# The matrices of a state-space layer, made two groups at a time: moved ahead of the stage that uses them

## The chip, the cores and the metric

One core of a Trainium2 chip runs the kernel. A core has five engines that each work through a queue of their own in order: TensorE (PE in the profile; its weight loads are PEld), VectorE (DVE), ScalarE (ACT), GpSimd (POOL) and SyncE (SP), which here mostly issues DMA transfers. They meet by semaphores. The metric is the device time of one execution in microseconds (us); less is better.

## What is computed

One layer of a decoder with 2048 positions of 1024 channels, in float32. The projection `P = rms_norm(x) @ W_in` feeds two attention mixers (columns a, b, c below) and a diagonal state-space mixer (columns u), and an output projection and a feed-forward block follow. The change lies in the projection and in the state-space mixer:

```python
A_bar = jnp.exp(A * dt)                       # 32 groups of 16 channels, 64 complex states each
B_bar = ((A_bar - 1.0) / A)[..., None] * Bm
Bu = jnp.einsum('blgp,gnp->blgn', uf.astype(jnp.complex64), B_bar)
_, states = lax.associative_scan(_scan_combine, (a_seq, Bu), axis=1)
y = jnp.einsum('blgn,gpn->blgp', states, Cm).real
y = y + d_skip.astype(f32).reshape(SSM_GROUPS, SSM_GROUP_CH) * uf
z = jax.nn.gelu(y.reshape(Bsz, L, W))
```

The kernel cuts the 2048 positions into 128 blocks of 16. Within a block the answer is a product with a lower triangular Toeplitz matrix of `C A^t B` (the local part); across blocks only the state at a block's edge is scanned, and it enters the answer through the matrices `C A^t`, t = 0 to 16.

## The kernel before

`phase_front` (L81) makes the projection. The positions are taken as 16 slices s of 128 rows; half 0 does s = 0 to 7, half 1 does 8 to 15. For a slice `load_h` (L99) loads x, transposes it on TensorE (tile pt, L111), splits it into a high and a low part (hh on ScalarE L113, hl on VectorE L114), squares x on ScalarE (L117, after which x's buffer is free; there are two) and makes the slice's row factor r, 1 over the root of the mean square, by `rsqrt_steps` (L41): eight instructions of 128x1, on GpSimd. `load_w` (L128) loads a chunk's weights and splits each of 8 parts into wh (ScalarE, L143) and wl (VectorE, L144). `product` (L150) then runs 24 matmuls for one slice and chunk (`mm3`: wh hh, wl hh, wh hl for 8 parts). ScalarE takes the result out with the factor r.

There are five chunks of columns: two of u (256 columns each), then a, b, c. In half 0 all five run, and beside u's second chunk to c the tables of the state-space part are made in 13 parts (`ssm_tables`, VectorE above all; AR and AI are the powers of A, C1 and C2 the coefficients C after a transposition on TensorE, tile p, L414; Ea and Eb the factors for turning states). In half 1 the two u chunks run first, so that u is complete; then a, b, c run merged with the state-space steps.

Those steps (`ssm_steps`, L430) treat the 32 groups as 16 pairs b. For a pair:

- `outer` (L460): CA = AR x C1 + AI x C2, 128x544, three GpSimd instructions L465 to L467;
- `local` (L470): pk, two matmuls of CA with the table Yp (L476); VectorE adds D (kst, L479), ScalarE copies the rest (L480), and SP stores kst to DRAM as a strip, dkp (L481), from which the Toeplitz matrix Wc is read back, shifted line by line (L490);
- `turned` (L483): the turns (six VectorE instructions L453 to L458 on t2u, into the factors E), B's matrices Bp (L494 to L496, VectorE), transposes of u (pu) and of Bp (pbt) on TensorE, and ScalarE's copies U and BT (L503, L508);
- `scanned` (L518): pv = BT times U on TensorE (L524), its halves swapped by ScalarE (vs, L515 and L516), m and the scan Q on VectorE (L527 to L533), the swap of Q on ScalarE (again L515 and L516), the states St on GpSimd (t, St, L536 and L537);
- `answer` (L539): py from Wc, U, CA and St, six TensorE instructions, and the activation into u_st.

CA has three buffers, so GpSimd runs up to two pairs ahead. Within the stage a pair's steps lie between halves of the products of a, b and c: `merge` deals the steps of several lists evenly into one order, and a scheduler then sets each engine's queue from that order, priorities and the buffers that come free. Waits go by semaphores on tiles; a load's wait for a free buffer stands in SP's queue and holds what is behind it.

Of the kernel before, what the change touches and what calls it, by code (L numbers as in the profile page):

```python
# [80 lines left out]
def phase_front(tc, C, x, norm1_g, w_in, u_st, pd, rh_a, prm, dkp, extra):  # L81

    nc = tc.nc
    with ExitStack() as ctx:
# [43 lines left out]
        def load_w(half, kind, c0, n):  # L128
# [301 lines left out]
def ssm_steps(tc, C, S, u_st, dkp, tp, ps, ps_t):  # L430
# [29 lines left out]
    def outer(b):  # L460

        bc = [P, GB, 17, 16]
        CA, t1 = tl(bc, "CA", b, 3), tl(bc, "t1", b)
        ar, ai = (S[n][:, :, of(b)].rearrange("p t g -> p g t").unsqueeze(3).broadcast_to(bc) for n in ("AR", "AI"))
        nc.gpsimd.tensor_tensor(CA, ar, S["C1"][:, of(b)].unsqueeze(2).broadcast_to(bc), op=ALU.mult)  # L465
        nc.gpsimd.tensor_tensor(t1, ai, S["C2"][:, of(b)].unsqueeze(2).broadcast_to(bc), op=ALU.mult)
        nc.gpsimd.tensor_tensor(CA, CA, t1, op=ALU.add)  # L467
        M["c", b] = CA

    def local(b):  # L470
# [1385 lines left out]
```

## Time and profile before

| | us |
|---|---|
| median of 3 runs | 2604.18 (2604.03 to 2604.61) |
| the profiled execution | 2609.15 |
| its span in the trace | 2607.0 |
| front phase (`phase_front`) | 0 to some 441 |
| half 0's chunk c | 144 to 179 |
| half 1's u chunks | 179 to 234 |
| SSM stage: a, b, c of half 1 with the 16 pairs | 234 to 441 |

Over the span TensorE is busy 2487.8 us (95%), VectorE 1802.0 (69%), ScalarE 1328.8 (51%), GpSimd 1141.6 (44%). These shares are means over stages with different limits. Read one stage by what its fullest engine waits for, then follow that wait to the engine that was late, and on that engine look for the instructions that took longer than others of their shape.

### The profile page before, as it was taken

The numbers are of one execution on the slowest core, as the hardware profiler recorded it, in microseconds if no ns is written. First come the engines' busy times: TensorE is split into PE (matmuls) and PEld (weight loads), VectorE is DVE, ScalarE is ACT, GpSimd is POOL, SyncE is SP. The second block draws the span as 40 slices with busy tenths as digits, with TensorE's granted clock in tenths as the row PEclk, the third lists the DMA queues.
The fourth block names the chain that finished last, engine by engine and source line by source line (L and its number), as shares of the span: only waits on it lengthen the run. The fifth ranks groups of instructions, "written<-read, shape, count | busy, mean of one in ns | idle before, by whom it ended". The sixth has DMA issues, their size and how long they took to land. (4 is left out here: it accounts for less than half of the span.)

```text
span 2607.0 us, 38424 instructions
## 1 busy us (share of the span) xinstructions
PE 2487.8 (95%) x12904; PEld 2089.8 (80%) x12904; DVE 1802.0 (69%) x3436; ACT 1328.8 (51%) x2774; POOL 1141.6 (44%) x1195
## 2 busy tenths in 40 slices
PE   8999989999899998999989999899999999999999
PEld 7999888777787777778868878688887888888887
DVE  3836876854776677787665655755557887888886
ACT  5344444854775656566545554544444443344442
POOL 2014544221333223333257666665564354454447
PEclk9999999999899999999989999999999999999999
DMA  4342214321312112112366666665546534444335
GB/s 124 88 140 76 73 51 123 118 76 48 106 56 69 52 49 84 61 52 69 100 198 191 189 197 193 203 182 152 154 134 219 179 115 133 130 128 128 120 102 197
DMA packets 393621, 316.78 MB, mean 122 GB/s; under 512 B 51494, under 2 KB 364460, under 8 KB 391600
## 3 DMA queue, kind: packets, MB, share of 16 engines
q1 hardware_dynamic: 357328, 289.16, 37.1%
q10 hardware_dynamic: 36096, 25.17, 3.0%
q8 instruction: 102, 1.67, 0.3%
q14 instruction: 95, 0.78, 0.1%
HBM read 206.26 MB, written 107.99 MB: 121 GB/s over the span
## 5 line engine op out<-in xcount | busy, mean ns | idle before, releaser
L1341 ACT CAST v<-vr 128x512 fp32r<-128x512 f32 x224 | 139.4, 624 | 307.8 <-DMA vr<-vd 150.0
L1342 DVE TENSOR_TENSOR v<-vr,v 128x512 fp32r<-128x512 f32 x224 | 239.6, 1078 | 77.8 <-ACT v L1341 74.9
L1656 PE MATMUL pdc<-dw,v 128*128 128x512 f32 x768 | 186.7, 392 | 4.9 <-ACT dw L1341 3.0
L1656 PE MATMUL pdb<-dw,v 128*128 128x512 f32 x768 | 184.6, 389 | 0.0
L1656 PE MATMUL pda<-dw,v 128*128 128x512 f32 x768 | 184.5, 389 | 0.0
L1656 PEld LDWEIGHTS pdc<-dw,v 128*128 128x128 f32 x768 | 145.0, 189 | 36.6 <-ACT dw L1341 3.4
L1452 POOL TENSOR_TENSOR fs<-ur,ur 128x512 f32<-128x512 f32 x64 | 94.0, 1469 | 171.5 <-DMA ur<-in_w_up 109.9
L1656 PEld LDWEIGHTS pdb<-dw,v 128*128 128x128 f32 x768 | 144.1, 188 | 30.3 <-ACT v L1341 0.4
L1656 PEld LDWEIGHTS pda<-dw,v 128*128 128x128 f32 x768 | 144.2, 188 | 29.9
L1341 ACT CAST uh<-fs 128x512 fp32r<-128x512 f32 x128 | 78.7, 621 | 150.9 <-PE pub L1481 63.3
L1342 DVE TENSOR_TENSOR ul<-fs,uh 128x512 fp32r<-128x512 f32 x128 | 131.9, 1034 | 22.7 <-ACT uh L1341 22.6
L1342 DVE TENSOR_TENSOR ul<-ur,uh 128x512 fp32r<-128x512 f32 x96 | 101.5, 1060 | 49.8 <-ACT uh L1341 43.5
L1497 POOL TENSOR_TENSOR ev<-e,e 128x512 f32<-128x512 f32 x64 | 98.9, 1545 | 38.5 <-ACT e L1494 23.2
L76 PE MATMUL pw<-wo_h,mh 128*128 128x512 f32 x256 | 110.4, 431 | 5.0 <-DVE ml L1211 2.5
L864 DVE TENSOR_TENSOR tls<-pps,ths 128x512 fp32r<-128x512 f32 (+1 forms) x144 | 92.8, 658 | 29.9 <-ACT ths L863 22.6
L863 ACT CAST ths<-pps 128x512 fp32r<-128x512 f32 (+1 forms) x144 | 79.1, 565 | 57.4 <-PE pps L860 27.5
L1481 PE MATMUL puc<-fl,uh 128*128 128x512 f32 x256 | 101.3, 396 | 4.8 <-DVE fl L1342 4.8
L1481 PE MATMUL pub<-fh,uh 128*128 128x512 f32 x256 | 102.9, 402 | 2.5 <-ACT fh L1341 2.5
L1481 PE MATMUL puc<-fh,uh 128*128 128x512 f32 x256 | 101.5, 397 | 3.9 <-ACT fh L1341 2.5
L77 PE MATMUL pw<-wo_l,mh 128*128 128x512 f32 x256 | 105.2, 411 | 0.0
L78 PE MATMUL pw<-wo_h,ml 128*128 128x512 f32 x256 | 104.8, 410 | 0.0
L1481 PE MATMUL pub<-fl,uh 128*128 128x512 f32 x256 | 102.3, 400 | 1.6 <-DVE fl L1342 1.6
(566 smaller groups left out, 7940.9 us busy)
## 6 DMA issues: line engine op xcount, KB each, us to landing
vr<-vd SPq DMA_DIRECT2D x224, 256.0 KB
ur<-in_w_up SPq DMA_DIRECT2D x128, 256.0 KB
vd<-ev SPq DMA_DIRECT2D x128, 256.0 KB
vd<-e ACTq DMA_DIRECT2D x64, 256.0 KB
dr<-in_w_down SPq DMA_DIRECT2D x32, 512.0 KB
x<-in_x SPq DMA_DIRECT2D x16, 512.0 KB
mx<-in_x SPq DMA_DIRECT2D x16, 512.0 KB
x<-mx ACTq DMA_DIRECT2D x16, 512.0 KB
```

The lines of the kernel that those rows point to most:

```text
L76: nc.tensor.matmul(out, sh, mh, start=first, stop=False)
L77: nc.tensor.matmul(out, sh, ml, start=False, stop=False)
L78: nc.tensor.matmul(out, sl, mh, start=False, stop=last)
L863: nc.scalar.copy(th[:, 0:nb], pt[:, 0:nb])
L864: nc.vector.tensor_tensor(tl[:, 0:nb], pt[:, 0:nb], th[:, 0:nb], op=ALU.subtract)
L1341: nc.scalar.copy(dh, src)
L1342: nc.vector.tensor_tensor(dl, src, dh, op=ALU.subtract)
L1452: nc.gpsimd.tensor_tensor(t, x, y, op=op)
L1481: nc.tensor.matmul(bank[b], w[:, k], h[o][:, k], start=first and k == 0 and n == 0, stop=k == HALF - 1 and n == 2, skip_group_check=True)
L1497: nc.gpsimd.tensor_tensor(tile_("v" + o), x, y, op=op)
L1656: nc.tensor.matmul(bank[b, q], x[:, q, j], y[:, j], start=first and j == 0 and n == 0, stop=j == 1 and n == 2, skip_group_check=True)
```

## The change

`outer` and `local` of all pairs leave `ssm_steps` for a new function, `pair_steps`, of 18 steps. Its first 8 steps (PAIRS_FIRST) are merged with half 0's chunk c, the other 10 with half 1's two u chunks. CA gets tiles of its own (oCA, four buffers) and goes to DRAM (dca, 278 KB a pair), two steps after it was made ("later stores"), as kst does. In the SSM stage `turned` reads CA back by a DMA. The turns of a pair now stand behind Bp, at the end of `turned`. The tables' 13 parts are dealt over u's second chunk, a and b alone, no longer over c too. The row factors of slices 8 to 15 are made on VectorE, not on GpSimd. Half 0's weight splits of a, b, c get a higher priority (W_HOIST).

```diff
-                rsqrt_into(nc, box_x[0], r, ss, 1.0 / D, 1, "rq", nc.gpsimd)
+                rsqrt_into(nc, box_x[0], r, ss, 1.0 / D, 1, "rq", nc.vector if s >= 8 else nc.gpsimd)
...
+                    with tc.high_priority(offset=W_HOIST) if kind in "abc" and not half else nullcontext():
+                        nc.scalar.activation(wh, raw[:, j], AF.Copy, scale=g1[:, k:k + 1])
+                        nc.vector.scalar_tensor_tensor(wl, raw[:, j], g1[:, k:k + 1], wh, op0=ALU.mult, op1=ALU.subtract)
...
-                run(lists[0] + (lists[1] + lists[2][:1] if half else []))
+                run(merge(lists[0] + lists[1], pairs[PAIRS_FIRST:]) + lists[2][:1] if half else lists[0])
...
-                run(merge(sum(lists[1:], []), [lambda: next(gen, None)] * TABLE_PARTS + [lambda: None] * TABLE_REST))
+                run(merge(sum(lists[1:4], []), [lambda: next(gen, None)] * TABLE_PARTS))
+                c_pre = ctx.enter_context(ExitStack())
+                pre = c_pre.enter_context(tc.tile_pool(name="pre", bufs=1, side="right", reuse_waits="tile"))
+                pairs = pair_steps(tc, C, S, dkp, dca, pre, ps_g)
+                run(merge(lists[4], pairs[:PAIRS_FIRST]))
             else:
+                c_pre.close()
...
-TABLE_REST = 3
+PAIRS_FIRST = 8
+W_HOIST = 300
...
+def pair_steps(tc, C, S, dkp, dca, tp, ps):
...
+    def outer(b):
+        bc = [P, GB, 17, 16]
+        CA = M["c", b] = tp.tile(bc, F32, tag="oCA", name=f"oCA{b}", bufs=4)
+        t1 = tp.tile(bc, F32, tag="ot", name=f"ot{b}", bufs=2)
...
+    def local(b):
...
+        kst = M["k", b] = tp.tile([16, GB, 256], F32, tag="kst", name=f"kst{b}", bufs=3)
...
+    def stored(b):
+        nc.sync.dma_start(dca[b], M.pop(("c", b)))
+        nc.sync.dma_start(dkp[group_slice(b), :, 112:368].rearrange("g q c -> q g c"), M.pop(("k", b)))
+
+    res = []
+    for b in range(NB + 2):
+        res.append(lambda b=b: (b > 1 and stored(b - 2), b < NB and outer(b), 0 < b <= NB and local(b - 1)))
+    return res
...
     def turned(b):
 
-        turns(b)
-        CA = M["c", b]
-        Wc = tl([P, GB, 256], "Wc", b, 2)
+        CA, Wc = tl([P, GB, 17, 16], "CA", b, 2), tl([P, GB, 256], "Wc", b, 2)
+        nc.sync.dma_start(CA, dca[b])
...
         M["b", b] = BT, U, CA, Wc
-        if b + 1 < NB:
-            outer(b + 1)
+        turns(b)
...
-    res = [first, lambda: turned(0)]
+    res = [lambda: None, lambda: turned(0)]
     for b in range(NB):
-        res += [lambda b=b: scanned(b), lambda b=b: next_(b)]
+        res += [lambda b=b: scanned(b), lambda b=b: b and answer(b - 1)]
```

The scheduler's result at three places follows; in these rows the line numbers of the kernel after are larger by 1 in the projection, by 7 in the tables and by 20 to 45 in the SSM steps, and the instructions of `outer` have become L452 to L454.

GpSimd in the SSM stage, before, around pairs 1 to 5 (CA and t<-k_AI are the outers; t<-Q and St the states):

```order
L536 TENSOR_TENSOR t_3128<-Q_3123,E_3058 128x4x127
L465 TENSOR_TENSOR CA_3207<-k_AR,k_C_725 128x544
L537 TENSOR_TENSOR St_2906<-t_3128 128x2x127
L467 TENSOR_TENSOR CA_3207<-CA_3207,t_3208 128x544
L466 TENSOR_TENSOR t_3322<-k_AI,k_C_726 128x544
L536 TENSOR_TENSOR t_3242<-Q_3237,E_3177 128x4x127
L465 TENSOR_TENSOR CA_3321<-k_AR,k_C_725 128x544
L537 TENSOR_TENSOR St_2905<-t_3242 128x2x127
L467 TENSOR_TENSOR CA_3321<-CA_3321,t_3322 128x544
L466 TENSOR_TENSOR t_3441<-k_AI,k_C_726 128x544
```

The same engine after, from the last two outers on:

```order
L452 TENSOR_TENSOR oCA_2773<-k_AR,k_C_726 128x544
L454 TENSOR_TENSOR oCA_2773<-oCA_2773,ot_2774 128x544
L452 TENSOR_TENSOR oCA_2886<-k_AR,k_C_726 128x544
L454 TENSOR_TENSOR oCA_2886<-oCA_2886,ot_2887 128x544
L556 TENSOR_TENSOR t_3215<-Q_3210,E_3177 128x4x127
L557 TENSOR_TENSOR St_3118<-t_3215 128x2x127
L556 TENSOR_TENSOR t_3316<-Q_3311,E_3273 128x4x127
L557 TENSOR_TENSOR St_3119<-t_3316 128x2x127
```

An outer's instructions stood between the states of every pair; now they are all done before the first state, and only t and St are left in the stage.

SyncE's queue with half 1's loads of x, before (x_2227 is slice 10, the next ones 11 and 12):

```order
L171 DMA pc<-po_c 128x398
L101 DMA x_2227<-in_x 128x1024
L137 DMA wr_u_4_2619<-in_w_in 128x256
L101 DMA x_2284<-in_x 128x1024
L137 DMA wr_u_5_2625<-in_w_in 128x256
L101 DMA x_2341<-in_x 128x1024
L101 DMA x_2398<-in_x 128x1024
```

And after (x_2351 is slice 10, then 11, 12, 13; oCA_2511 is pair 11, oCA_2607 pair 12, kst_2238 pair 7):

```order
L101 DMA x_2351<-in_x 128x1024
L469 DMA dkp<-kst_2238 16x2x256
L468 DMA dca<-oCA_2511 128x544
L101 DMA x_2408<-in_x 128x1024
L137 DMA wr_u_4_2808<-in_w_in 128x256
L469 DMA dkp<-kst_2348 16x2x256
L468 DMA dca<-oCA_2607 128x544
L101 DMA x_2478<-in_x 128x1024
L137 DMA wr_u_5_2814<-in_w_in 128x256
L101 DMA x_2548<-in_x 128x1024
```

Before, only loads stood between loads of x; now the stores of CA of pair 11 and of kst of pair 7 stand ahead of slice 11's load, those of pairs 12 and 8 ahead of slice 12's, and so on.

VectorE in half 1's first u chunk, before (hl of slices 9 and 10, with two weight splits):

```order
L114 TENSOR_TENSOR hl_2173<-pt_0_2174,hh_2172 128x512
L144 SCALAR_TENSOR_TENSOR wl_u_2_2610<-wr_u_2_2607,g_111,wh_u_2_2609 128x256
L114 TENSOR_TENSOR hl_2173<-pt_1_2181,hh_2172 128x512
L144 SCALAR_TENSOR_TENSOR wl_u_3_2616<-wr_u_3_2613,g_111,wh_u_3_2615 128x256
L114 TENSOR_TENSOR hl_2230<-pt_0_2231,hh_2229 128x512
L114 TENSOR_TENSOR hl_2230<-pt_1_2238,hh_2229 128x512
```

And after (hl of slice 9, the row factors of slices 8 and 9, rqh, rqt and r, and the splits and pk's step between them):

```order
L114 TENSOR_TENSOR hl_2284<-pt_0_2285,hh_2283 128x512
L49 TENSOR_SCALAR r_2217<-rqt,r_2217 128x1
L48 TENSOR_SCALAR rqt<-r_2217,rqh 128x1
L114 TENSOR_TENSOR hl_2284<-pt_1_2292,hh_2283 128x512
L49 TENSOR_SCALAR r_2217<-rqt,r_2217 128x1
L48 TENSOR_SCALAR rqt<-r_2217,rqh 128x1
L44 TENSOR_SCALAR rqh<-ss_2299 128x1
L49 TENSOR_SCALAR r_2217<-rqt,r_2217 128x1
L45 TENSOR_SCALAR r_2301<-rqh 128x1
L145 SCALAR_TENSOR_TENSOR wl_u_2_2799<-wr_u_2_2796,g_112,wh_u_2_2798 128x256
L48 TENSOR_SCALAR rqt<-r_2301,rqh 128x1
L145 SCALAR_TENSOR_TENSOR wl_u_3_2805<-wr_u_3_2802,g_112,wh_u_3_2804 128x256
```

Where VectorE had the hl of one slice after another, eight small instructions of a row factor now come between them, and a kst for a pair. TensorE's queue has a pk (two matmuls) in each c product of half 0 and about one in each slice of the u chunks, and none in the SSM stage, where every pair had one.

## Rows read from the trace of the kernel before

**Rows 1.** Busy time of each engine (with its number of instructions), granted clock of TensorE (1.00 is full speed), busy share of the DMA engines and their GB/s, in four stretches: half 0's chunk c, half 1's first u chunk, the next chunk's start, the SSM stage. Columns: PE busy (x) PEld busy (x) DVE busy (x) ACT busy (x) POOL busy (x), PEclk, DMA share, GB/s.

```profile
144.00:179.00 35.00, 35.00 (x195) 35.00 (x195) 7.67 (x20) 12.61 (x28) 0.00 (x0) 1.00 0.40 126
179.00:211.00 32.00, 30.32 (x255) 29.49 (x254) 12.66 (x22) 22.06 (x45) 18.42 (x64) 1.00 0.41 122
211.00:222.00 11.00, 11.00 (x95) 11.00 (x94) 3.69 (x10) 5.28 (x10) 0.20 (x1) 1.00 0.36 99
234.00:441.00 207.00, 189.26 (x1095) 179.75 (x1094) 155.82 (x291) 90.67 (x195) 94.88 (x75) 0.96 0.25 72
```

**Rows 2.** What TensorE waited for in the SSM stage, 234 to 441 us: its line, the releaser, us in all, times, longest.

```profile
PE pv L524 <- ACT BT L508: 13.6, 7, 4.8
PE pm_a L77 <- DVE wl_a L144: 2.1, 1, 2.1
PE pm_a L76 <- ACT wh_a L143: 2.0, 1, 2.0
```

**Rows 3.** One of these waits, in the order of time, 338 to 348 us (start us, us, engine, line, op, tiles; in brackets the idle time before and what ended it).

```profile
338.77 1.42 POOL L467 TENSOR_TENSOR CA<-CA,t 128x544 f32<-128x544 f32 x1
338.89 1.57 DVE L457 TENSOR_TENSOR t2u<-k_Ea,k_Eb 128x256 f32<-128x256 f32 x1
...
344.24 0.40 ACT L515 COPY Q<-Q 64x256 f32<-64x256 f32 x1 [6.96 <-DVE kst L479]
...
346.80 0.56 ACT L508 COPY BT<-pbt 128x512 f32<-128x512 f32 x1
...
347.41 0.58 PE L524 MATMUL pv<-U,BT 128*128 128x128 f32 x1 [4.85 <-ACT BT L508]
```

**Rows 4.** As group 1, for two short stretches of the SSM stage.

```profile
241.00:248.00 7.00, 5.03 (x18) 4.54 (x18) 2.25 (x5) 3.35 (x7) 0.00 (x0) 0.53 0.41 114
347.00:351.00 4.00, 3.59 (x15) 3.59 (x16) 3.79 (x10) 1.09 (x3) 0.20 (x1) 0.57 0.38 113
```

**Rows 5.** VectorE in order of time, start of the SSM stage: one product of the turns beside GpSimd's outers, a sum of the same shape and a product of 128x512 with GpSimd idle (its L466 from 235.34 lasts 1.24 us).

```profile
222.27 1.40 DVE L454 TENSOR_TENSOR t2u<-k_Ea,k_Eb 128x256 f32<-128x256 f32 x1
...
236.90 0.42 DVE L455 TENSOR_TENSOR E<-t2u 128x256 f32<-128x256 f32 x1
...
238.61 0.69 DVE L495 TENSOR_TENSOR t<-k_AI,k_W 128x512 f32<-128x512 f32 x1
```

**Rows 6.** VectorE's instructions on the tiles t2u and E of the turns (L453 to L458) in the SSM work, 222 to 441 us: span, busy (x), PEclk, DMA share, GB/s.

```profile
222.00:441.00 219.00, 63.51 (x96) 0.96 0.25 70
```

**Rows 7.** VectorE's three instructions of Bp, 222 to 441 us, by line and shape: busy us, mean ns of one, idle time before.

```profile
L494 DVE TENSOR_TENSOR Bp<-k_AR,k_Y 128x512 f32<-128x512 f32 x16 | 17.9, 1119 | 15.8 <-PE pbt L506 15.8
L496 DVE TENSOR_TENSOR Bp<-Bp,t 128x512 f32<-128x512 f32 x16 | 17.4, 1087 | 0.3
...
L495 DVE TENSOR_TENSOR t<-k_AI,k_W 128x512 f32<-128x512 f32 x16 | 12.7, 791 | 0.1
```

**Rows 8.** The same view of GpSimd, 222 to 441 us.

```profile
L467 POOL TENSOR_TENSOR CA<-CA,t 128x544 f32<-128x544 f32 x16 | 24.6, 1538 | 0.6
L536 POOL TENSOR_TENSOR t<-Q,E 128x508 f32<-128x508 f32 x16 | 22.8, 1426 | 106.2 <-ACT Q L516 106.2
L465 POOL TENSOR_TENSOR CA<-k_AR,k_C 128x544 f32<-128x544 f32 x16 | 22.7, 1422 | 10.8 <-DVE gate L201 10.8
L466 POOL TENSOR_TENSOR t<-k_AI,k_C 128x544 f32<-128x544 f32 x16 | 21.1, 1319 | 1.1
L537 POOL TENSOR_TENSOR St<-t 128x254 f32<-128x254 f32 x16 | 15.2, 953 | 0.7
```

**Rows 9.** All instructions that read or write the tiles pk (local products on TensorE, and VectorE's and ScalarE's steps from them to kst), 222 to 441 us: PE busy (x) PEld busy (x) DVE busy (x) ACT busy (x), PEclk, DMA share, GB/s.

```profile
222.00:441.00 219.00, 16.42 (x64) 12.12 (x64) 2.67 (x16) 8.66 (x16) 0.96 0.25 70
```

**Rows 10.** Half 1's loads of x on SyncE's queue, and the transposes on TensorE that wait for x, in order of time.

```profile
186.02 1.07 PE L111 MATMUL pt<-c_ident,x 128*128 128x128 f32 x8 [0.33 <-DMA x<-in_x]
...
188.84 11.84 SPq L101 DMA_DIRECT2D x<-in_x  x4
...
193.81 1.07 PE L111 MATMUL pt<-c_ident,x 128*128 128x128 f32 x8 [0.85 <-DMA x<-in_x]
```

**Rows 11.** What TensorE waited for from 73 to 234 us.

```profile
PE pm_b L77 <- DVE wl_b L144: 1.4, 1, 1.4
PE pt L111 <- DMA x<-in_x: 1.2, 2, 0.8
```

**Rows 12.** A one-operand VectorE instruction of 128x96 at two times: with GpSimd in L466 (319.32 to 320.48), and with GpSimd idle.

```profile
319.39 1.15 DVE L53 TENSOR_SCALAR hnhn<-hnhn 128x96 f32<-128x96 f32 x1
...
321.46 0.21 DVE L53 TENSOR_SCALAR hnhn<-hnhn 128x96 f32<-128x96 f32 x1
```

**Rows 13.** Half 0's chunk b, in order of time: a load of B and its use, the last load of C, C's transposes, and two matmuls of the product.

```profile
124.73 1.36 SPq L385 DMA_DIRECT2D t_B<-in_ssm_b_im  x1
...
129.51 0.34 PE L76 MATMUL pm_b<-wh_b,hh 128*128 128x384 f32 x1
...
129.68 0.34 PE L77 MATMUL pm_b<-wl_b,hh 128*128 128x384 f32 x1
...
129.84 0.42 DVE L397 TENSOR_SCALAR t_B<-t_B 64x512 f32<-64x512 f32 x1 [0.46 <-DMA t_B<-in_ssm_b_im]
129.85 0.51 SPq L393 DMA_DIRECT2D craw<-in_ssm_c_re  x1
...
139.46 1.04 PE L414 MATMUL p<-c_ident,craw 128*128 128x128 f32 x8
```

More of the change, by code (lines that the diff above doesn't have):

```diff
@@ L210, in phase_front @@
                 rest = sum(lists[2:], [])[1:]
-                run(merge(rest, ssm_steps(tc, C, S, u_st, dkp, tp, ps_g, ps_t)))
+                run(merge(rest, ssm_steps(tc, C, S, u_st, dkp, dca, tp, ps_g, ps_t)))
                 store(0)
@@ L427, with group_slice, ssm_steps @@
 GB = 2
-def ssm_steps(tc, C, S, u_st, dkp, tp, ps, ps_t):
+def group_slice(b):
+    return slice(b * GB, b * GB + GB)
+def pair_steps(tc, C, S, dkp, dca, tp, ps):
+    nc = tc.nc
+    M = {}
+    NB = G // GB
+    def outer(b):
+        bc = [P, GB, 17, 16]
+        CA = M["c", b] = tp.tile(bc, F32, tag="oCA", name=f"oCA{b}", bufs=4)
+        t1 = tp.tile(bc, F32, tag="ot", name=f"ot{b}", bufs=2)
+        ar, ai = (S[n][:, :, group_slice(b)].rearrange("p t g -> p g t").unsqueeze(3).broadcast_to(bc) for n in ("AR", "AI"))
+        nc.gpsimd.tensor_tensor(CA, ar, S["C1"][:, group_slice(b)].unsqueeze(2).broadcast_to(bc), op=ALU.mult)
+        nc.gpsimd.tensor_tensor(t1, ai, S["C2"][:, group_slice(b)].unsqueeze(2).broadcast_to(bc), op=ALU.mult)
+        nc.gpsimd.tensor_tensor(CA, CA, t1, op=ALU.add)
+    def local(b):
+        CA = M["c", b]
+        pk = ps.tile([P, GB, 256], F32, tag="pb", name=f"pk{b}", bufs=2)
+        for i in range(GB):
+            g = b * GB + i
+            nc.tensor.matmul(pk[:, i], S["Yp"][:, g:g + 8].rearrange("p a b -> p (a b)"), CA[:, i, 0:16].rearrange("p a b -> p (a b)"),
+                             start=True, stop=True)
+        kst = M["k", b] = tp.tile([16, GB, 256], F32, tag="kst", name=f"kst{b}", bufs=3)
+        nc.vector.tensor_tensor(kst[:, :, 0:16], pk[0:16, :, 0:16], S["dD"][:, group_slice(b)], op=ALU.add)
+        nc.scalar.copy(kst[:, :, 16:256], pk[0:16, :, 16:256])
+    def stored(b):
[5 more added lines that the diff above has]
+    return res
+def ssm_steps(tc, C, S, u_st, dkp, dca, tp, ps, ps_t):
     nc = tc.nc
@@ L437, in ssm_steps @@
     NB = G // GB
+    of = group_slice
     def tl(shape, n, b, bufs=1):
         return tp.tile(shape, F32, tag=n, name=f"{n}{b}", bufs=bufs)
-    def of(b):
-        return slice(b * GB, b * GB + GB)
     def turns(b):
@@ L458, in turns @@
         nc.vector.tensor_tensor(o[1], u1, u2, op=ALU.add)
[L460 to L470, printed above, removed]
-        CA = M["c", b]
-        pk = ps.tile([P, GB, 256], F32, tag="pb", name=f"pk{b}", bufs=2)
-        for i in range(GB):
-            g = b * GB + i
-            nc.tensor.matmul(pk[:, i], S["Yp"][:, g:g + 8].rearrange("p a b -> p (a b)"), CA[:, i, 0:16].rearrange("p a b -> p (a b)"),
-                             start=True, stop=True)
-        kst = tl([16, GB, 256], "kst", b)
-        nc.vector.tensor_tensor(kst[:, :, 0:16], pk[0:16, :, 0:16], S["dD"][:, of(b)], op=ALU.add)
-        nc.scalar.copy(kst[:, :, 16:256], pk[0:16, :, 16:256])
-        nc.sync.dma_start(dkp[of(b), :, 112:368].rearrange("g q c -> q g c"), kst)
     def turned(b):
-        turns(b)
-        CA = M["c", b]
-        Wc = tl([P, GB, 256], "Wc", b, 2)
+        CA, Wc = tl([P, GB, 17, 16], "CA", b, 2), tl([P, GB, 256], "Wc", b, 2)
+        nc.sync.dma_start(CA, dca[b])
         for i in range(GB):
@@ L546, in answer @@
         nc.scalar.activation(u_st[:, of(b)], py, AF.Gelu_apprx_tanh)
-    def first():
-        outer(0)
-        local(0)
-    def next_(b):
-        if b:
-            answer(b - 1)
-        if b + 1 < NB:
-            local(b + 1)
-    res = [first, lambda: turned(0)]
+    res = [lambda: None, lambda: turned(0)]
     for b in range(NB):
-        res += [lambda b=b: scanned(b), lambda b=b: next_(b)]
+        res += [lambda b=b: scanned(b), lambda b=b: b and answer(b - 1)]
         if b + 1 < NB:
```

7 lines of the change are left out of this document (3 added, 4 removed).

## The prediction

> **What bounds the kernel now.** I read the page first (TensorE 95% busy over the span), then the busy time of each engine by stage, then TensorE's waits in the stage that the change touches, then the engines that these waits lead to. The edit lies in the front phase, 0 to 441 us; what follows keeps its instructions, so I only ask when the front phase ends.
>
> The stage table [rows 1] splits it. Half 0's chunk c (144 to 179) has TensorE without a gap and GpSimd without one instruction. Half 1's first u chunk (179 to 211) and second (211 to 222 and on) are TensorE's too. The SSM stage (234 to 441) is different: TensorE is busy 189.26 of 207 us, at a mean granted clock of 0.96. TensorE's waits there [rows 2] sum to 13.6 + 2.1 + 2.0 = 17.7 us, and 13.6 of it is one thing: pv waits for ScalarE's copy BT, 7 times. One of the seven in full [rows 3]: VectorE's state factors (t2u, E) run beside GpSimd's outer products; the product L457 takes 1.57 us while GpSimd is in L467. ScalarE's Q swap has stood still 6.96 us behind the late VectorE, the copy BT stands behind the swap on ScalarE (in order), and pv has waited 4.85 us when it starts.
>
> The clock is the second part. Mean 0.96 over 207 us, with levels 1 and 0.5 of full speed, is 207 x 0.04 / 0.5 = 16.6 us at the lower level (1.2 GHz), so 8.3 us lost. The stretches with 0.53 and 0.57 [rows 4] lie right behind such a wait (347 to 351 starts where pv waited 4.85 us).
>
> Why VectorE is late shows in one op at two times [rows 5]: the sum L455, 128x256, takes 0.42 us when GpSimd is idle; L454, the same shape, takes 1.40 us at 222.27, with GpSimd's outers running back to back. Over the stage the 96 ops of the turns take 63.51 us [rows 6] instead of 96 x 0.42 = 40.3, and the three Bp products [rows 7] 17.9 + 12.7 + 17.4 = 48.0 instead of 48 x 0.69 = 33.1 (L495 with GpSimd idle, [rows 5]): 23.2 + 14.9 = 38 us of VectorE go into waiting for GpSimd.
>
> **The change part by part.** *SSM stage.* The outers (L465 to L467) leave it: 22.7 + 21.1 + 24.6 = 68.4 us of GpSimd, 4.28 a pair [rows 8]; with them go those 38 us of VectorE. What stays on GpSimd is t and St, 22.8 + 15.2 = 38.0 us [rows 8], which can still block VectorE. So VectorE falls from 155.82 of 207 us busy [rows 1] to some 120, and the local product, its addition and its copy (16.42 us TensorE, 2.67 VectorE, 8.66 ScalarE for 16 pairs [rows 9]) leave as well. TensorE becomes the only full engine of the stage. The gain is at most 17.7 + 8.3 = 26.0 us. It isn't all had: the 4.1 us of waits for the first a casts [rows 2] don't come from the outers, and ScalarE still has the swap ahead of BT. I keep a quarter: **-19.6**. Bounds: all of it, -26.0; half of it, -13.0 (the nearest row against me is t and St, over half as long as the outers).
>
> *The local products pk.* 16.42 us of TensorE leave the SSM stage and come back in chunk c (pairs 0 to 7) and the u chunks, where TensorE has no gap [rows 1]: **0** net. Nothing hides them there.
>
> *The outers in their new place.* Eight run beside chunk c, 8 x 4.28 = 34 us in a stretch of 35 in which GpSimd had nothing and VectorE 7.67 us [rows 1]: that is the cover, and pair b is wanted once a c product (35/8 = 4.4 us and its pk), so the pace fits. Eight more run beside u1 and u2. There SP's queue now holds the x loads behind the stores of CA. In u1 TensorE needs 32/8 = 4.0 us a slice [rows 1], its waits for x in it, and now 16.42/16 = 1.0 more for pk, some 4.9; GpSimd needs 4.28 a pair. So the pace fits but the phase is tight: x is used 193.81 - 188.84 = 5.0 us after its issue [rows 10], TensorE already waits 0.33 and 0.85 us for it, and the store of pair 11, 12 x 4.28 = 51 us after the start of the outers at about 137 (C's data near 135, below, then its copies on VectorE), lets slice 11's load go at 188.4, where it went at 188.84. Each late microsecond of the start is one on x. Besides, the u weights' second parts, two-operand VectorE ops, can each wait up to 1.4 us like L454 [rows 5], and hl of slice 8 stands behind six of them. From slice 12 on there is also a loop: x of slice b waits for the store of CA b, that for outer b, that (four buffers) for pk b-4, and TensorE reaches pk b-4 two slices before x of b: 1.0 + 4.28 + 5.0 = 10.3 us for two slices, against TensorE's 9.8, about even. I take **+4**. Bounds: -1.2 (the waits for x vanish, as the pk give each load more time; [rows 11]) and +15 (first rival, in full).
>
> *Row factors on VectorE.* Eight 128x1 ops for each of 8 slices leave GpSimd, 18.42 us for the 64 [rows 1]; GpSimd would else need 4.28 + 2.3 a slice, more than TensorE. On VectorE (12.66 us busy of 32) they add some 64 x 0.2 = 13 us: an estimate from the small op of [rows 12] without GpSimd beside it, 0.21. Covered, if they aren't blocked.
>
> *Tables earlier, b's and c's casts earlier.* Two terms, one on the other. The waits for wl_b (1.4, [rows 11]) may go. But C's transposes, at 139.46 behind the seventh b product, now stand three matmuls into the sixth: 45 matmuls earlier, at 0.17 each [rows 13] 7.7 us, so at 131.8 or, without the waits, 130.4. Their data can't be there: the loads of B and C wait for VectorE's last use of a table's space, which the new order has at the same place. A load of B issued at 124.73 was used at 129.84; the last of C, issued at 129.85, then lands near 135. That is a stall of 3.2 against the old time. I take **+2.5**; bounds -1.4 (the casts' wait gone, C small and early) and +3.2.
>
> *CA through DRAM.* 16 stores and 16 loads of 128x544 (278 KB each). The loads are issued a pair ahead of py; the DMA engines are 25% busy in the stage [rows 1], 41% at most in the stretches shown [rows 4]. **0**, and up to +1 if the first is late; the turns, now behind Bp, are also no longer the first thing that pbt waits for.
>
> **Sum:** -19.6 + 4 + 2.5 = -13.1 against the profiled execution's 2609.15: 2596.0. That execution is 5.0 above the median of the three runs (2604.18), and one execution doesn't tell in which stage, so the difference goes to the median: **2591**.
>
> **Rivals.** *The row factors are blocked in u1.* Beside GpSimd's L466 a one-operand TENSOR_SCALAR of 128x96 took 1.15 us, alone 0.21 [rows 12]. If the 128x1 ops wait like it, each of GpSimd's three ops a pair stops one of them: 3 x 1.4 + 5 x 0.2, two hl at 0.7 and a kst, 6.8 us a slice against TensorE's 4.9, with the hl that TensorE wants queued behind them: 8 x 1.9 = +15 in place of my +4, so -19.6 + 15 + 2.5 = -2, **2602**. For it: that row; against it: one element a partition is a very small transfer, and no row has it beside a long GpSimd op. The Trainium skill (SBUF — State Buffer, "Who interferes with whom") has the same lock on the port pair that VectorE shares with GpSimd, held for a whole instruction, for two-operand ops and for tensor_scalar in its two-port modes; by it this rival would hold wherever such a mode is taken, and the traced 1.15 agrees with it, while no run here shows it for one element. The page also says that whoever issues first holds the pair; by that GpSimd could be the blocked one, and the outers late.
>
> *The waits stay.* BT stays behind the swap on ScalarE and TensorE's stream between pbt and pv stays 12 matmuls long (2.1 us at 0.17), so half of the 26 stays whatever VectorE does: -13 + 6.5 = -6.5, **2598**. Against it: the swap was late because of VectorE's blocked ops [rows 3].
>
> *Slower: the queue of x loads.* The loop above (pk b-4, outer b, store of CA b, x of b, two slices on) sets the pace when its parts stretch: each of the outer's three ops waits for a VectorE op of up to 0.7 (hl), 4.28 + 2.1 = 6.4; x lands in 10 us instead of 5.0 since the stores share its DMA engines; with pk 17.4 for two slices, 8.7 for one, 3.8 over TensorE's 4.9. For slices 10 to 15 that is +23 in place of my +4: -19.6 + 23 + 2.5 = +6, **2610**. It decides from a loop of some 17 us up. For it: TensorE waits for x at two places already, and SP issues in order. Against it: GpSimd's ops hardly stretch beside a full VectorE (the means of [rows 8] are 1.32 to 1.54, in a stage where VectorE is 75% busy), and the DMA engines have room.
>
> That the change doesn't do what it says is excluded by the order: no outer and no pk stands in the SSM stage any more.
>
> **How the numbers follow.** Forecast 2591, chance 0.62; row factors blocked 0.13 (2602); waits stay 0.15 (2598); queue 0.10 (2610). The forecast's best end, all bounds at once, is -26.0 - 1.2 - 1.4 = -28.6: 2575.6; its worst without the rivals -13 + 4 + 3.2 = -5.8: 2598. Rival one lies within 2604, the slow one beyond. **Range 2577 to 2604.** A change of under 0.2% (5.2 us, so 2599.0 to 2609.4) can't be told from none: faster 0.72 (the forecast's 0.60 and most of the waits' case), the same 0.20 (most of the first rival's, a part of each other one), slower 0.08.
>
> **What would show it.** Right: in the SSM stage TensorE's wait for BT is under 5 us, its clock 0.98 or more, the turns' ops at 0.42 to 0.5, and the stage is some 35 us shorter (of which 16 are pk, paid earlier). Chunk c and u1 each some 8 us longer. A stall of 2 to 3 us before C's transposes near 132. Wrong: VectorE's 128x1 ops at over 0.5 us in u1 and TensorE waiting for hl; waits for x over 6 us; waits for BT still near 13 us with a quick VectorE, which would say that ScalarE's order, not GpSimd, made them.

## The result and the profile after

The median fell from 2604.11 us (2602.09 to 2604.61, 4 runs) to 2582.47 (2580.45 to 2590.4, 4 runs): a ratio of 0.9924, 95% interval 0.9902 to 0.9946, some 21.6 us less. A second series of the same kernel, beside other runs of the kernel before (2605.68), gave 2585.54 and 0.9923 (0.9911 to 0.9935).

Where it came from is read off TensorE, whose work kept its order of chunks: the start of the first or last matmul of a tile, in us from the span's start.

| | before | after | difference | this stretch alone |
|---|---|---|---|---|
| half 0: first matmul of chunk b | 107.6 | 106.6 | -1.0 | -1.0 |
| first of chunk c | 144.5 | 146.2 | +1.6 | +2.6 |
| last of chunk c | 179.0 | 187.7 | +8.7 | +7.1 |
| half 1: first of chunk a (u chunks done) | 234.4 | 250.7 | +16.2 | +7.5 |
| last of chunk c (SSM stage done) | 440.3 | 418.5 | -21.7 | -37.9 |
| span's end | 2607.0 | 2578.7 | -28.4 | -6.7 |

Up to the end of the front phase the profiled executions differ by -21.7, as the medians do. The 6.7 after it belong to the two executions, not to the change: in a second trace of the kernel after, the front phase ends at 418.8 and the rest takes 2586.0 - 418.8 = 2167.2, as before (2607.0 - 440.3 = 2166.7); in the first it took 2160.2. In all the traces below, whose programs differ only ahead of it, this rest takes 2160.1 to 2171.0. So the last c matmul of half 1 is the finer measure, and the experiments are read by it.

The stages of the kernel after (the columns are those of [rows 1]): a stretch of chunk b, one of chunk c, and the SSM stage.

```profile
130.00:140.00 10.00, 8.28 (x42) 8.22 (x43) 7.07 (x11) 1.00 (x2) 4.43 (x4) 0.83 0.60 122
144.00:179.00 35.00, 34.18 (x186) 33.09 (x185) 10.99 (x22) 12.05 (x26) 28.91 (x24) 1.00 0.60 197
250.70:419.00 168.30, 166.26 (x1027) 160.75 (x1026) 116.74 (x271) 83.32 (x179) 36.49 (x35) 1.00 0.36 105
```

In the SSM stage TensorE is busy 166.26 of 168.30 us at a clock of 1.00, where it had 189.26 of 207 at 0.96 [rows 1]; VectorE has fallen from 155.82 to 116.74 us, GpSimd from 94.88 to 36.49. GpSimd now works in chunk c (28.91 us). The stretch 130 to 140 has a clock of 0.83 in this trace, and of 1.00 in the second trace of the same kernel.

TensorE's waits, first ahead of the SSM stage, then in it, answer to [rows 2, 11]:

```profile
PE p L421 <- DMA craw<-in_ssm_c_im: 2.9, 1, 2.9
PE pt L111 <- DMA x<-in_x: 1.6, 1, 1.6
PE pm_c L77 <- DVE wl_c L145: 0.8, 1, 0.8
PE pm_b L77 <- DVE wl_b L145: 0.4, 1, 0.4
...
PE pv L544 <- ACT BT L529: 2.0, 3, 0.9
```

The 13.6 us for BT have become 2.0, and those for a's first splits are gone. New are 2.9 us for C's data (tile p) and 0.8 for a split of c's weights (wl_c); the wait for x is 1.6 (1.2 before), that for wl_b 0.4 (1.4).

The turns, as in [rows 6], and GpSimd's outers at their new place, as in [rows 8]:

```profile
250.00:419.00 169.00, 36.16 (x90) 1.00 0.36 105
```

```profile
L454 POOL TENSOR_TENSOR oCA<-oCA,ot 128x544 f32<-128x544 f32 x16 | 22.1, 1382 | 0.9
...
L452 POOL TENSOR_TENSOR oCA<-k_AR,k_C 128x544 f32<-128x544 f32 x16 | 19.6, 1231 | 112.1 <-DVE k_C L425 93.1 <-PE pk L461 19.0
L453 POOL TENSOR_TENSOR ot<-k_AI,k_C 128x544 f32<-128x544 f32 x16 | 19.2, 1208 | 0.9
```

90 ops of the turns take 36.16 us, 0.40 each, where 96 took 63.51. An outer takes 1.23 + 1.21 + 1.38 = 3.8 us (4.28 before), and GpSimd waits 19.0 us in all for pk.

The question of the first rival, VectorE's row factors beside the outers, stands in one stretch of the u chunks, both engines in order of time:

```profile
191.13 1.35 POOL L454 TENSOR_TENSOR oCA<-oCA,ot 128x544 f32<-128x544 f32 x1
...
191.39 0.28 DVE L48 TENSOR_SCALAR rqt<-r,rqh 128x1 f32<-128x1 f32 x1
...
192.20 0.20 DVE L49 TENSOR_SCALAR r<-rqt,r 128x1 f32<-128x1 f32 x1
...
192.44 0.27 DVE L48 TENSOR_SCALAR rqt<-r,rqh 128x1 f32<-128x1 f32 x1
...
192.56 1.18 POOL L453 TENSOR_TENSOR ot<-k_AI,k_C 128x544 f32<-128x544 f32 x1
...
193.23 0.20 DVE L49 TENSOR_SCALAR r<-rqt,r 128x1 f32<-128x1 f32 x1
```

GpSimd is in L454 from 191.13 to 192.48 and in L453 from 192.56 to 193.74; the row factor's instructions run inside both, and across the step from one to the other, at 0.20 to 0.28 us each.

### The profile page after: what moved, and what is told of

Its sections match the earlier page's. It is cut to its first block, busy times and chain, and to the rows that moved or that the text cites. A ratio compares the mean times of both kernels' runs of the same rounds, so it can differ in the third digit from the quotient of the medians.

```text
span 2578.7 us, 38486 instructions
## 1 busy us (share of the span) xinstructions
PE 2476.0 (96%) x12904; PEld 2081.5 (81%) x12904; DVE 1781.8 (69%) x3500; ACT 1329.8 (52%) x2774; POOL 1115.2 (43%) x1131
## 5 line engine op out<-in xcount | busy, mean ns | idle before, releaser
L1352 DVE TENSOR_TENSOR ul<-fs,uh 128x512 fp32r<-128x512 f32 x128 | 138.1, 1082 | 22.6 <-ACT uh L1351 22.6
L1491 PE MATMUL pua<-fh,uh 128*128 128x512 f32 x256 | 100.8, 394 | 2.2 <-ACT e L1511 2.2
```

The costliest lines, as they stand in the source:

```text
L1352: nc.vector.tensor_tensor(dl, src, dh, op=ALU.subtract)
L1491: nc.tensor.matmul(bank[b], w[:, k], h[o][:, k], start=first and k == 0 and n == 0, stop=k == HALF - 1 and n == 2, skip_group_check=True)
```

## The experiments

Theory: GpSimd's outers made VectorE's two-operand ops wait, VectorE made ScalarE's swap and BT late, TensorE waited and its clock fell. The rivals are named at each run. "Front" is the start of half 1's last c matmul (before 440.3, after 418.5 and 418.8); the ratio is that to the kernel before, run beside it.

| run | front | SSM stage (first a to last c) | median, us | ratio, 95% interval |
|---|---|---|---|---|
| after | 418.5 | 167.9 | 2582.47 | 0.9924 (0.9902 to 0.9946) |
| after, again | 418.8 | 168.6 | 2585.54 | 0.9923 (0.9911 to 0.9935) |
| outers_twice | 451.6 | 201.7 | 2621.26 | 1.0051 (1.0035 to 1.0066) |
| outers_twice_turns_first | 454.6 | 203.5 | 2624.46 | 1.0067 (1.0050 to 1.0085) |
| gpsimd_fills | 427.6 | 173.8 | 2593.64 | 0.9948 (0.9931 to 0.9966) |
| turns_first | 418.3 | 167.4 | 2588.33 | 0.9933 (0.9913 to 0.9953) |
| pk_in_stage | 432.9 | 179.8 | 2600.51 | 0.9972 (0.9962 to 0.9982) |
| pk_in_stage_stores_on_gpsimd | 438.6 | 180.6 | 2607.87 | 1.0007 (0.9998 to 1.0017) |
| factors_on_gpsimd | 423.3 | 168.3 | 2590.27 | 0.9937 (0.9922 to 0.9952) |
| casts_not_hoisted | 430.1 | 168.4 | 2599.20 | 0.9977 (0.9967 to 0.9987) |
| c_transposes_later | 420.6 | 168.9 | 2586.43 | 0.9926 (0.9909 to 0.9943) |
| c_later_x_on_scalare | 414.8 | 167.7 | 2582.70 | 0.9912 (0.9899 to 0.9926) |
| c_later_stores_on_gpsimd | 414.9 | 168.3 | 2583.30 | 0.9916 (0.9902 to 0.9929) |

**The kernel after, again.** Nothing is edited.

> The kernel after, unchanged, a second time. Its front phase should end within 1.5 us of the first time (last c product of half 1 at 418.5 us). If the later phases, which the change leaves as they were, differ by several us between executions of one kernel, the 7 us by which they were shorter in the first trace of after than in the trace of before are such a difference and no part of the gain.

The front phase ended at 418.8 us, 0.3 from the first time, and the rest took 7 us more than then: the difference after the front phase is none of the change's.

**The outers back in the stage.**

```diff
 def stored(b):
-    nc.sync.dma_start(dca[b], M.pop(("c", b)))
...
 def turned(b):
-    nc.sync.dma_start(CA, dca[b])
+    CA = M["c", b]
...
     turns(b)
+    if b + 1 < NB:
+        outer(b + 1)       # the three GpSimd products of before, L465 to L467
```

The early outers stay, since pk needs them, but CA is neither stored nor loaded.

> The kernel after, but the SSM stage makes its CA again with three GpSimd products a pair, as the kernel before did, and no longer loads it; the early outers, pk and kst stay early. Theory (GpSimd's outers hold up VectorE's two-operand ops, so that TensorE waits for BT and the clock falls): the turns' ops are back at a mean of 0.55 to 0.95 us, TensorE's waits for BT at 8 to 18 us, the granted clock of the stage at 0.95 to 0.98, and the time 12 to 22 us above the kernel after. Rival (the gain is that pk, kst and their ScalarE copy left the stage): waits under 5 us, clock at 1.00, the time of the kernel after within 4 us.

The SSM stage took 201.7 us, 33.9 more than in the kernel after. The stage, then the turns, then TensorE's waits:

```profile
249.90:451.60 201.70, 176.72 (x1025) 168.09 (x1024) 163.08 (x278) 82.39 (x178) 96.70 (x78) 0.94 0.23 69
```

```profile
250.00:451.00 201.00, 64.84 (x94) 0.94 0.23 69
```

```profile
PE pv L553 <- ACT BT L536: 18.7, 8, 5.6
PE pm_a L77 <- DVE wl_a L145: 5.0, 1, 5.0
PE pm_a L76 <- ACT wh_a L144: 1.1, 1, 1.1
```

The turns are back at 64.84 us for 94 ops (0.69 each), the waits at 24.8 us, the clock at 0.94, and VectorE and GpSimd work about as long as before (163.08 and 96.70 us, against 155.82 and 94.88). The account closes: 22.8 us more waiting, and 201.7 x 0.06 / 0.5 = 24 us at the lower level of the clock, 12 of them lost, make 35, against 33.9 measured. The theory holds; its size was expected too small: 12 to 22 us for the time, which is 33 to 39 above the kernel after, 8 to 18 us of waiting for BT, which is 18.7, and a clock of 0.95 to 0.98, which is 0.94. I had taken the kernel before less pk as the measure. The stage is nearly as long as before (205.8) though pk is out of it. I read this as VectorE's chain setting its length while the outers are in it, with pk lying in TensorE's waits: the waits are 7.1 us longer than the 17.7 of before, and the clock costs 4 more. No run tests that reading by itself.

The u chunks, which have no stores of CA here, take 62.9 us with 1.5 us of waiting for x, as in the kernel after (62.9 and 1.6). So the stores cost TensorE nothing there.

**GpSimd as busy, but not reading.**

```diff
+def outer(b):
+    CA = M["c", b] = tl([P, GB, 17, 16], "CA", b, 3)
+    for _ in range(8):
+        nc.gpsimd.memset(CA, 0.0)
...
     nc.sync.dma_start(CA, dca[b])      # overwrites the zeros
```

> The kernel after, with GpSimd kept busy in the SSM stage by eight fills (memset, 128x544) of the CA tile of each pair ahead of its load: no reading of SBUF, about the time of an outer. Theory (it is the outers' reading of SBUF that VectorE's two-operand ops wait for): turns' ops stay at 0.42 to 0.5 us, waits for BT under 6 us, within 5 us of the kernel after. Rival (GpSimd's time itself, its states t and St coming late behind other work): waits for BT or py of 8 us and more with quick turns' ops, and 8 to 20 us above the kernel after.

The stage, the turns, GpSimd's fills (as in [rows 8]) and the wait:

```profile
254.00:427.00 173.00, 168.09 (x1020) 162.73 (x1019) 117.39 (x271) 83.41 (x178) 96.50 (x147) 0.98 0.36 105
```

```profile
254.00:427.00 173.00, 36.07 (x90) 0.98 0.36 105
```

```profile
L508 POOL MEMSET CA<- 128x544 f32 x120 | 65.8, 553 | 5.1
```

```profile
PE pv L551 <- ACT BT L534: 4.9, 3, 2.1
```

GpSimd is busy 96.50 us in the stage, as with the outers (96.70), and the turns stay at 36.07 us. So it is what the outers read, not GpSimd's time, that VectorE waits for. GpSimd's time has a price of its own, 5 to 6 us of stage against the two traces of the kernel after: 2.1 to 2.9 more of waiting for BT, and some 3 by the clock (173 x 0.02 / 0.5 / 2). Another 3 lie ahead of the stage, where the wait for x was 3.5; nothing was edited there, and why it grew isn't shown. The whole time missed the expectation of "within 5 us": it is 8 to 11 above the kernel after, in the range that the rival had given, though without the rival's sign, a wait of 8 us.

**The order of the turns.**

```diff
 def turned(b):
+    turns(b)
...
     M["b", b] = BT, U, CA, Wc
-    turns(b)
```

> The kernel after with the turns at the head of a pair's steps again, ahead of Bp. Theory (GpSimd's outers made VectorE late, not the order of its work): waits for BT under 6 us, the granted clock at 0.99 to 1.00, the time within 4 us of the kernel after. Rival (Bp was late because it stood behind the turns): waits for BT of 7 us and more, 8 to 16 us above the kernel after.

> The run outers_twice with the turns at the head of a pair's steps again, so that the SSM stage has the work of the kernel before without pk and kst. If the order of the turns makes the difference between outers_twice's stage (201.7 us) and that of the kernel before less pk (206 - 16 = 190): 187 to 194 us from the first a product of half 1 to the last c product. If not (early pk and kst change the order of ScalarE or VectorE to the worse): 197 to 206.

Waits of turns_first, then of outers_twice_turns_first, from 255 to 420 us:

```profile
PE pv L544 <- ACT BT L530: 1.8, 3, 0.8
```

```profile
PE pv L553 <- ACT BT L537: 17.0, 8, 5.2
PE pm_a L77 <- DVE wl_a L145: 6.2, 1, 6.2
```

turns_first ends the front phase 0.2 us before the first trace of the kernel after, and its stage has a clock of 1.00; its median, 3 to 6 us above, can't be told from that of the kernel after (the intervals overlap). The order of the turns is worth nothing, with the outers gone. With them back it doesn't explain the length of outers_twice either (203.5 against 201.7); over the whole stage the wait for BT is 18.0 us in 9 times, and the first a splits cost 7.2. The rival falls on both.

**The local products back in the stage.**

```diff
 def next_(b):
     if b:
         answer(b - 1)
+    if b + 1 < NB:
+        local(b + 1)      # from a CA that a DMA reads back, three buffers
```

> The kernel after with the local products (pk, kst and their store) back in the SSM stage, fed by CA that is loaded from DRAM; the outers alone are early. Theory (the outers' leaving is the gain): the stage is longer by pk's 14 to 17 us and chunk c and the u chunks shorter by as much, waits for BT under 6 us, the time within 4 us of the kernel after. Rival (pk's and kst's leaving is the gain): waits for BT of 8 us and more, and 10 to 20 us above the kernel after.

The stage:

```profile
253.00:433.00 180.00, 179.26 (x1090) 172.90 (x1090) 119.22 (x287) 91.00 (x194) 35.78 (x35) 1.00 0.36 103
```

In the stage the theory holds: TensorE is full (179.26 of 180.00), at a clock of 1.00, the wait for BT is 0.7, and it is longer by 12.0, which is pk: less than the 14 to 17 expected from its 16.42 us of busy time. But the front phase ends 14.4 later than in the kernel after, and by the whole time I would have to prefer the rival. The loss lies in the u chunks, which take 70.9 us with no pk in them, against 62.9 with nine; between 188 and 211 us TensorE's clock is 0.65. TensorE's waits there, and the queues of SyncE and ScalarE behind them:

```profile
PE pm_u L76 <- ACT hh L113: 7.5, 1, 7.5
PE pt L111 <- DMA x<-in_x: 5.0, 1, 5.0
```

```profile
190.27 6.60 SPq L457 DMA_DIRECT2D dca<-oCA  x3
...
201.06 0.51 ACT L144 ACTIVATE wh_u<-wr_u,g 128x256 fp32r<-128x256 f32 x1 [7.69 <-DMA wr_u<-in_w_in]
201.47 0.56 ACT L113 CAST hh<-pt 128x512 fp32r<-128x512 f32 x1
```

With no pk to wait for, the outers and their stores were ordered ahead of the loads: ScalarE waited 7.69 us for a part of the u weights that stood on SyncE behind three stores of CA (6.60 us from the first to the last), and the cast hh, for which TensorE waited, stood behind it on ScalarE. That is the hazard of the slow rival, stores ahead of loads on SyncE, in a kernel where it happens; the rival's loop isn't there, since it ran through pk.

To take it away, the stores went to GpSimd's queue:

```diff
-nc.sync.dma_start(dca[b], M.pop(("c", b)))
+nc.gpsimd.dma_start(dca[b], M.pop(("c", b)))
```

> The run pk_in_stage with the stores of CA issued from GpSimd's queue, so that no load stands behind them on SyncE. Theory (there the loss was the loads of x and of the u weights behind the stores): no waits of TensorE for x or u weights over 2 us in the u chunks, the stage unchanged at 178 to 182 us, front phase within 5 us of the kernel after. Rival (pk's place as such costs the 14 us): front phase 10 us and more above the kernel after.

```profile
PE pt L111 <- DVE hl L114: 11.1, 1, 11.1
PE pm_c L77 <- DVE wl_c L145: 5.7, 2, 2.9
```

```profile
250.00:440.00 190.00, 188.24 (x1159) 181.01 (x1157) 121.87 (x294) 94.06 (x202) 36.13 (x35) 1.00 0.35 98
```

In the u chunks the waits for x and the weights are gone, and the stage is as it was. But the front phase ends 20 us after that of the kernel after, where the theory had 5 at most: TensorE waits 11.1 us for hl, and in chunk c 5.7 us for splits of c's weights. VectorE's weight splits of 128x256 stood ahead of it, five in 14.5 us. One of them, and GpSimd beside it:

```profile
188.76 4.02 DVE L145 SCALAR_TENSOR_TENSOR wl_u<-wr_u,g,wh_u 128x256 fp32r<-128x256 f32 x1
...
188.89 1.37 POOL L454 TENSOR_TENSOR oCA<-oCA,ot 128x544 f32<-128x544 f32 x1
190.21 1.17 POOL L452 TENSOR_TENSOR oCA<-k_AR,k_C 128x544 f32<-128x544 f32 x1
191.34 1.16 POOL L453 TENSOR_TENSOR ot<-k_AI,k_C 128x544 f32<-128x544 f32 x1
192.45 0.58 POOL L457 DMA_DIRECT2D dca<-oCA  x1
```

It is a two-operand op of 0.48 us when nothing is beside it, and it took 4.02: it spans three GpSimd products without a gap and ends inside the DMA issue behind them. The pace of the outers alone doesn't do that. In pk_in_stage they were as dense and as little held back by pk, with their stores on SyncE, and no split of the u weights beside them took more than 1.58 us. In c_later_stores_on_gpsimd (below), where pk does pace them but GpSimd issues the stores, one took 2.88. So this run doesn't show either that pk's place is free; it shows that GpSimd's outers with their stores on GpSimd's own queue can hold VectorE up in the u chunks too. Whether an early outer with a late pk could match the kernel after stays open.

**Row factors on GpSimd.**

```diff
-rsqrt_into(nc, box_x[0], r, ss, 1.0 / D, 1, "rq", nc.vector if s >= 8 else nc.gpsimd)
+rsqrt_into(nc, box_x[0], r, ss, 1.0 / D, 1, "rq", nc.gpsimd)
```

> The kernel after with the row factors of slices 8 to 15 on GpSimd again. If GpSimd's pace sets the u chunks (an outer of 3.7 us and 2.3 to 2.9 of a factor for a slice of 4.6 us): outers late, x loads late behind CA's stores, TensorE's waits for x of 6 us and more, 6 to 15 us above the kernel after. Rival (the move to VectorE does nothing, GpSimd has room and the outers wait for pk anyway): within 3 us of the kernel after.

```profile
PE pt L111 <- DMA x<-in_x: 4.5, 2, 3.4
```

The u chunks take 4.4 us longer (67.4 against 62.9), the wait for x is 4.5 us, the front ends 4.8 later, and the median is 5 to 8 us above those of the kernel after. So the move to VectorE is worth some 5 us, a little less than expected (6 to 15, with a wait for x of 6 or more).

**Weight splits without their priority.**

```diff
-with tc.high_priority(offset=W_HOIST) if kind in "abc" and not half else nullcontext():
+with nullcontext():
```

> The kernel after without the higher priority of half 0's weight splits: in VectorE's order wl_b 4 to 7 then stand behind most of the tables. Theory (the tables, dealt over fewer products, would hold them up): TensorE waits 4 to 12 us for wl_b in chunk b, C's transposes wait less, and the time is 3 to 10 us above the kernel after. Rival (the splits have room anyway): within 2 us.

```profile
PE pm_a L77 <- DVE wl_a L145: 4.1, 1, 4.1
PE pm_c L76 <- ACT wh_c L144: 3.7, 1, 3.7
PE pm_b L77 <- DVE wl_b L145: 1.6, 2, 1.1
PE pm_c L77 <- DVE wl_c L145: 1.3, 3, 0.7
```

The front phase ends 11.6 us later, more than the 3 to 10 expected: 10.7 us of waits in half 0's chunks a to c, though only 1.6 of them at wl_b, where I had expected 4 to 12. With the tables dealt over fewer products, the priority is what keeps the splits in time; C's data is no longer waited for.

**C's transposes later.**

```diff
-run(merge(sum(lists[1:4], []), [lambda: next(gen, None)] * TABLE_PARTS))
+run(merge(sum(lists[1:4], []) + lists[4][:2], [lambda: next(gen, None)] * TABLE_PARTS))
...
-run(merge(lists[4], pairs[:PAIRS_FIRST]))
+run(merge(lists[4][2:], pairs[:PAIRS_FIRST]))
```

> The kernel after with the tables' parts dealt over chunk c's first two steps too and the pairs over the rest of c, which puts C's transposes behind b's sixth product, some 4 us later in TensorE's queue. If the stall for C's data is all there is to it: no wait for craw, chunk c starts 2.5 to 4.5 us earlier, and the front phase ends 2 to 4 us earlier than in the kernel after. Rival (the outers then start later and what is won is lost again to waits for pk, x or the weights): the end within 1.5 us of the kernel after, or later.

```profile
PE pt L111 <- DMA x<-in_x: 2.9, 1, 2.9
PE pm_u L76 <- ACT hh L113: 1.3, 1, 1.3
PE pm_c L76 <- ACT po_c L168: 1.0, 1, 1.0
```

The wait for C's data is gone and chunk c starts at 143.4, 2.8 us earlier than in the first trace of the kernel after and 1.3 earlier than in the second (144.7). But the front phase ends 1.8 to 2.1 later: TensorE waits 2.9 us for x, and 2.3 for hh and po_c. The rival holds. Two runs keep this edit and take the loads of x and the stores of CA apart. The first issues the loads from ScalarE's queue, the second the stores from GpSimd's, as above:

```diff
-nc.sync.dma_start(xt, xv[s])
+(nc.scalar if s >= 10 else nc.sync).dma_start(xt, xv[s])
```

> The run c_transposes_later with half 1's loads of x from slice 10 on issued from ScalarE's queue, which frees x's buffer itself. Theory (what the later transposes won was lost to loads of x behind CA's stores): no wait for x over 1 us, the front phase ends 3 to 6 us before that of the kernel after. Rival (the issue on ScalarE delays its casts, or pk waits instead): within 2 us of it or later.

> The run c_transposes_later with the stores of CA issued from GpSimd's queue. Theory as for the x loads on ScalarE: no wait for x over 1 us, the front phase ends 3 to 6 us before that of the kernel after. Rival (GpSimd's own part of a transfer slows the outers): outers over 4.5 us a pair with their stores, TensorE waits for pk, and the end within 2 us of the kernel after or later.

Waits of c_later_x_on_scalare ahead of the stage:

```profile
PE pm_u L76 <- ACT hh L113: 1.3, 1, 1.3
PE pm_c L76 <- ACT po_c L168: 1.0, 1, 1.0
PE pm_b L77 <- DVE wl_b L145: 0.6, 1, 0.6
```

No wait for x is left, and the front phase ends at 414.8, 3.7 to 4.0 before the kernel after; with the stores on GpSimd's queue it ends at 414.9. By the front phase both are the best of the versions run. The second owes part of that to its start: its chunk b begins at 104.8, 1.8 to 2.1 us before those of the kernel after. From there to the end of the front phase it is 1.9 us shorter than the kernel after, the first 4.6, and in the u chunks it waits 3.5 us for hh: ScalarE stands behind a kst that VectorE makes late, after six weight splits in 7.46 us, one of them of 2.88. Its outers take some 4.6 us a pair with their stores, which was the rival's sign, but TensorE waits for no pk. By their medians they can't be told from the kernel after (0.9912 and 0.9916 against 0.9923, the intervals overlap).

## Why the prediction was right, and where its terms were off

The time lay in the range, the sign was right, and the sum was 8.6 us short. By stretches (pk taken as in the prediction, 16.42 / 16 each; by the order seven of them lie in chunk c and nine in the u chunks, where the prediction had eight and eight):

| stretch | predicted | measured | second trace |
|---|---|---|---|
| ahead of chunk b | 0 | -1.0 | -0.7 |
| chunk b | +2.5 | +2.6 | +0.8 |
| chunk c (seven pk) | +7.2 | +7.1 | +7.4 |
| u chunks (nine pk, and +4) | +13.2 | +7.5 | +8.2 |
| SSM stage (-16.4 and -19.6) | -36.0 | -37.9 | -37.2 |
| sum | -13.1 | -21.7 | -21.5 |

The price of pk hides how far the terms were off. Its matmuls are busy for 16.41 us in the trace of after, as before, but they lengthen a stretch by less: in pk_in_stage all sixteen cost the stage 12.0 us, or 13.3 with the 1.3 us by which the wait for BT was shorter, and chunk c, without its seven, is 5.4 shorter. That is 0.75 to 0.83 us each, not 1.03. At that price some 24 to 26 of the 37 to 38 us that left the SSM stage are waits and clock, and what the u chunks took beyond their nine pk is 0 to 1.5 us.

- *What bounds the SSM stage.* Right, and shown: the outers put back cost 33.9 us of stage, the same GpSimd time without reading 5 to 6, the order of the turns nothing.
- *"I keep a quarter."* This term was mis-sized most: -19.6 where 24 to 26 were had. Of 26.0 us of waits and clock, 2.0 of waiting and none of the clock's are left. The reason that I gave for keeping a quarter, ScalarE's swap ahead of BT, still stands in the order, but the waits that it leaves are 2.0 us. The waits for the first a splits, which I thought were none of the outers' doing, went too, came back in outers_twice (5.0 + 1.1) and were therefore theirs. "The waits stay" falls with it.
- *The u chunks, +4.* Almost nothing was to be added, 0 to 1.5. The waits there were 1.6 for x and 0.4 for hl, against 1.2 for x and 0.5 for hl and hh before. I had let the loop of stores and loads (10.3 us for two slices) stand against TensorE's 9.8 as if even meant late. It didn't set the pace: GpSimd stood 19.0 us waiting for pk, and without any store of CA (outers_twice) the u chunks are as long and wait as long for x. The wait for x itself can grow, as pk_in_stage, factors_on_gpsimd and c_transposes_later show at 5.0, 4.5 and 2.9 us.
- *Row factors on VectorE, the first rival.* False: in the stretch shown they run inside reading GpSimd products at 0.20 to 0.28 us, and the 24 of L48 and 24 of L49 of the whole u chunks have means of 0.27 and 0.21. What a 128x96 op of the same kind suffered [rows 12] doesn't carry over to 128x1. Nor were the outers late: an outer took 3.8 us. The move had its worth in GpSimd's room, some 5 us.
- *Tables earlier, splits earlier, +2.5.* The stall came where it was forecast, 2.9 us up to 131.7 (2.5 in the second trace), and wl_b's wait fell from 1.4 to 0.4. That chunk b then measured +2.6 is luck: the second trace has +0.8. The clock makes the difference, and the term had none of it: behind the wait it is 0.83 from 130 to 140 us in the first trace, which is 1.7 us lost (10 x 0.17 / 0.5 / 2), and 1.00 in the second. Nine of the traces of the kernel after and its versions have this wait, of 2.5 to 3.2 us. In five of them the clock is 0.83 there and chunk b takes 39.2 to 39.8 us, in four it is 1.00 and chunk b takes 37.6 to 37.8 (36.9 before). Without the priority of the splits the earlier tables would have cost 11.6 more.
- *CA through DRAM, 0.* No wait of TensorE names CA in the trace of after.
- *The chunk c.* The cover named, GpSimd's empty 35 us, held: 28.91 us of outers there, and c is longer by 7.1. Of that 5.4 are its pk; pk_in_stage, which has the outers but no pk there, keeps the other 1.7, with 0.8 of it as a wait for wl_c.

The Trainium skill (SBUF — State Buffer, "Who interferes with whom") says that a VectorE op with two SBUF inputs contends with a GpSimd instruction that reads SBUF, and not with one that only writes it. gpsimd_fills and outers_twice agree: 36.07 and 64.84 us of turns beside 96.5 us of GpSimd work each.

## What to carry to other kernels

When an engine's two-operand ops take thrice their length in one stage, look at what GpSimd reads at that time before giving either engine less work: moving GpSimd's reading out of the stage where VectorE is wanted was worth more than all the instructions moved with it. Look at the new place too: in chunk c VectorE had 7.67 us of work in 35, and in the u chunks the hl that TensorE wants, of which one operand is TensorE's own result pt, took 0.69 us with the outers beside it as without. Watch the pace of such early work (here the wait for pk) and the queue that its stores stand in: they can stand ahead of the loads that the next stage wants, as in pk_in_stage. Price a moved instruction by what its removal gives (here some 0.8 us a pk), not by its busy time. And judge a front-phase change by the start of a matmul behind it, since the rest of this program differed between executions by a third to a half of such a gain.

## What the runs showed of the hardware

- A GpSimd memset of 128x544 (0.55 us, 120 of them) doesn't slow VectorE's two-operand ops (0.40 us an op of the turns); a GpSimd product of the same tile does (0.69).
- VectorE's one-operand ops of 128x1 are untouched by a reading GpSimd product (0.20 to 0.28 us inside one of 1.35), those of 128x96 are not (1.15 against 0.21, [rows 12]).
- A two-operand VectorE op can wait for more than one GpSimd instruction: 4.02 us for a 128x256 split beside three products and a DMA issue of GpSimd's own queue. In the kernel after, whose outers had no DMA issue among them, such splits took at most 1.43 us, in pk_in_stage, also without, 1.58, and with the issues in c_later_stores_on_gpsimd 2.88. Why the issue makes the difference isn't settled.
- One and the same wait of TensorE, 2.5 to 3.2 us in chunk b, was followed by a mean clock of 0.83 over 130 to 140 us in five traces and of 1.00 in four, two of the nine being of one kernel.
